# Splitting the experts' weights a whole 128x2048 unit at a time, with 8 KB places for the parts

## The chip, the cores and the metric

The kernel runs on one core of one Trainium2 chip. The metric is device time in microseconds (us) of one execution, and the median of the runs is compared. TensorE is called PE in the profile (PEld is its weight load), VectorE DVE, ScalarE ACT, GpSimd POOL; SP is the engine on whose queue the kernel issues its loads. The granted TensorE clock is 1.00 in nearly the whole profile; in the stretches of 5 us from 525 to 540 us, from the router into the experts, it is 0.65, 0.50 and 0.83.

## What is computed

Two layers of a decoder trunk for 256 tokens of width 1024, in float32. Layer 0 is a token mixer and a dense channel mixer; layer 1 is a token mixer and eight experts, of which each token takes two:

```python
def moe_swiglu(h, router_w, w_gate, w_up, w_down):
    t = h.reshape(B * S, D)
    logits = (t @ router_w).astype(jnp.float32)
    top_v, top_i = lax.top_k(logits, TOP_K)
    top_w = jax.nn.softmax(top_v, axis=-1)
    gates = jnp.sum(jax.nn.one_hot(top_i, N_EXPERTS) * top_w[..., None], axis=1)
    for e in range(N_EXPERTS):
        y = y + gates[:, e:e + 1] * swiglu(t, w_gate[e], w_up[e], w_down[e])
```

with `swiglu(h, g, u, d) = (silu(h @ g) * (h @ u)) @ d`, a width of 3584 inside, and a final RMSNorm. All weights are read once from HBM, 479 MB in all; the experts' are 336 loads of 1 MB.

## The kernel before, in words

**The products.** A float32 product is made of three products of float32r parts: with a weight w = hi + lo and an input x = hi + lo, PE does x_hi·w_hi, x_hi·w_lo and x_lo·w_hi. In the experts (`experts`, L854) the inputs are the stationary operand (128x128: `xe_hi`, `xe_lo` in `wide`, L990; `g_hi`, `g_lo` in `down`, L1028) and the weights are the moving one, 512 columns at a time. Each of the 8 experts is worked through in 7 chunks of 512 inner columns. A chunk is, in PE's order: the gate product (24 matmuls), with the turning of the chunk before put in after step k = 5 (`turn`, L1009: 4 transposes, then ACT's `g_hi` and DVE's `g_lo`); the up product (24); the down product of the chunk before (24). An expert's tokens are gathered ahead of it (`gather`, L968), its rows put back in small jobs (`finish`, L1046). The order within an engine is that of the code.

**The weights' way.** `Stream` (L81) brings them: `load` issues a load of one unit (128x2048 float32, 8 KB in each partition) when a load place is free; a unit holds two pieces of 1024 columns. `prep` has ACT copy a piece to its float32r part (L139: `w`, the hi); `rest` has DVE subtract it from the raw piece (L159: `lo`); when DVE has subtracted the last piece of a unit, the load place is free. A piece serves 6 matmuls. `get` hands out the next piece, and before that prepares ahead as far as places are free; `pump` prepares up to a number of pieces, with `lazy` their hi alone.

**The places.** Loads have 14 places of 8 KB in the experts: 8 of the pool `raws`, 3 of `raws2`, and the three tiles `q`, `k` and `v` of the pool `qkv`, which the mixer of layer 1 no longer needs (`ws.extend`, L788 and L791). Hi parts have 5 places of 4 KB: four of the pool `splits` and, since the mixer of layer 1, one of the pool `accs` (`ws.widen`, L1274); they are taken in turn, so that every fifth piece of the experts, beginning with the first, has its hi in `accs`. Lo parts have four of `splits`. The pools lie behind each other in memory in the order in which they are opened (L211 to L219, then L1278 on). In the built program the places of `splits` start 32 bytes past a multiple of 64, those of `accs` and the tiles `q`, `k` and `v` (all of the pools `accs` and `qkv`) at a multiple of 64. The stationary tiles of the experts (`xe_hi`, `xe_lo`, `g_hi`, `g_lo`) start 32 bytes past a multiple of 64, those of the dense mixer's down product and of the mixers (`dg_hi`, `dg_lo`, `onT_hi`, `onT_lo`) at a multiple of 64.

**The change over to the experts.** The mixer of layer 1 ends in `close` (L440), where `row_r` calls `ws.rest` (L460) just ahead of the second `diag`, which the transposes for the router wait for. In the router two pieces get their hi ahead (L929, L959); between them stands the branch of `overflow` (L1170), which all engines pass. `ws.rest(2)` (L962) stands in the middle of the eight subtractions of `xn[2]` (L964).

Of the kernel before, what the change touches and what calls it, by code (L numbers as in the profile page):

```python
# [44 lines left out]
# columns of the packed per-partition vectors, per layer  # L45
V_ADAB, V_ATTN, V_FFN, V_QN, V_KVN, V_OUT, V_FB = 0, 48, 56, 64, 66, 67, 75
V_LAYER = 76
# columns of the shape constants
# [6 lines left out]
# sections of the conditioning that are gates, the first section, and those whose sums wait for a time when  # L55
# the products' engine is free
# [6 lines left out]
# the channel blocks in the order in which they are modulated, those of a pair from different banks  # L63
NATURAL = ((0, 1), (2, 3), (4, 5), (6, 7))
PAIRS = ((0, 2), (1, 3), (4, 6), (5, 7))
# steps of the values' products that are followed by the first scores
# [13 lines left out]

class Stream:  # L81
    """Weights in the order of their use: loaded ahead, then split into two float32r parts.

    sources: of each unit, the address and the elements per partition. pieces: (unit, offset, what)
    in order, of SPLIT elements each; those with a `what` are folded into the conditioning instead."""

    def __init__(self, nc, sources, pieces, raw_pool, split_pool, fold):
        self.nc, self.sources, self.pieces = nc, sources, pieces
        self.raw_pool, self.split_pool, self.fold = raw_pool, split_pool, fold
        self.left = [0] * len(sources)  # L90
        for u, *_ in pieces:
            self.left[u] += 1
        self.raw, self.pool_of, self.bufs = {}, {}, RAW_BUFS
        self.loaded = self.oldest = self.next_prep = 0
        self.prepped = self.given = self.released = 0
        self.ready, self.late, self.late_by = [], [], 6
        self.turns, self.low_turns = ([(split_pool, tag, SPLIT_BUFS)] * SPLIT_BUFS for tag in ("whi", "wlo"))
        self.halves, self.held = [], {}

    def extend(self, raws):  # L100
        """Further places for loads, of pools and tags, which follow the others in turn."""
        for place in raws:
            self.pool_of[self.loaded] = place
            self.bufs += 1
            self.load()

    def widen(self, pool, tag):
        """A further place for a first part, which is the next in turn."""
        self.turns.insert(0, (pool, tag, 1))
# [14 lines left out]
    def prep(self, lazy=False):  # L124
        u, o, what = self.pieces[self.next_prep]
        self.load()
        raw = self.raw[u][:, o:o + SPLIT]
        i = self.next_prep
# [8 lines left out]
        else:  # L137
            hi = self.place(self.turns, f"w{i}")
# [4 lines left out]
            self.halves.append((u, raw, self.ready[-1]))  # L143
            self.prepped += 1

    def place(self, turns, name):
        turns.append(turns.pop(0))
        pool, tag, bufs = turns[-1]
        return pool.tile([P, SPLIT], F32R, tag=tag, name=name, bufs=bufs)

    def rest(self, n=None):
        """The second parts of the first n pieces that are ready: a step after the first parts, on
        another engine, which so need not wait for them."""
        n = len(self.ready) if n is None else n
        while (len(self.ready) - len(self.halves) < n and
               self.prepped - len(self.halves) < self.released + len(self.low_turns)):
            u, raw, parts = self.halves.pop(0)
            parts.append(self.place(self.low_turns, "lo"))
            self.nc.vector.tensor_sub(parts[1], raw, parts[0].bitcast(F32))  # L159
            self.used(u)  # L160
# [5 lines left out]
    def pump(self, most=None, need=0, lazy=False):  # L166
        """Prepare ahead: up to `most` pieces, as far as their places are free; lazy: only their first parts."""
        n = 0
        while self.next_prep < len(self.pieces) and (most is None or n < most):
            if self.pieces[self.next_prep][2] is None:  # L170
                ahead = len(self.turns) - (self.prepped >= self.given + need)
                if self.prepped >= self.released + ahead:
                    break
# [3 lines left out]
    def idle(self, most):  # L177
        """All uses of the pieces given have been issued; prepare some more."""
# [15 lines left out]
    def get(self, n=1):  # L194
        """The next pieces, once all uses of those given before have been issued."""
# [8 lines left out]


@with_exitstack
def trunk_kernel(ctx: ExitStack, tc: tile.TileContext, x, c, positions, w_early, w_moe, router_w,
# [5 lines left out]
    split_pool = ctx.enter_context(tc.tile_pool(name="splits", bufs=SPLIT_BUFS))  # L213
# [61 lines left out]
    def fold(w, l, section, k):  # L275
        """A part of a section of the conditioning: of the gates one row of eight, acc[p] += c[8 p + k] *
        w[8 p + k]; of the others a block of the channels, whose rows are the partitions. The blocks of
        the very first section are sums by the products' engine."""
        if (l, section) == FIRST:
            ps = bank("A", [P, P], "ps_fold")  # L280
            for i in range(KD):
                # a column and zeros: 128 columns cost less than one
# [9 lines left out]
        if k == 0:  # L292
            # the last may begin while the one before is held, after the last use of the conditioning's rows
# [9 lines left out]
        def done():  # L303
            """The sum over the partitions; what is returned puts it in its place."""
# [36 lines left out]
    for y in order:  # L341
        pieces.append((*place[y], y[1:] if y[0] == "ada" else None))
# [14 lines left out]
    def row_r(ss, n, name, between=None):  # L357
        """(sum of ss / n + eps) ** -0.5, of the rows' sums of squares; `between` goes where the
        vector engine waits for the last of them."""
# [17 lines left out]
    def turned(src, b, dg, ps, pairs=NATURAL):  # L377
        """The transpose of 128 rows times the diagonal, into PSUM [channel, 2, token] by pairs."""
# [24 lines left out]
    def modulated_T(l, at_g, sc, sh, ps, hi, lo):  # L403
        """The modulated rows, in two parts. Of each pair of blocks two engines make one each."""
# [15 lines left out]
    def first_modulated_T(ps, hi, lo, steps):  # L420
        """The very first of them, block after block as the conditioning comes in; steps: of how many
        blocks, and what brings theirs. The last parts of a step come after the folds of the next."""
# [17 lines left out]
    def close(l, section, acc, parts, n, table=None, spare=None, pairs=PAIRS, early=0):  # L440
        """x += gate row * acc, where parts(i, b, columns) are the last n steps of the sums acc[b];
        a quarter after the other, so that the next norm starts early. Its transpose and rstd. The sum
        of the held section `spare` goes where the products' engine waits for the last quarter."""
# [45 lines left out]
    def column_products(hT_hi, hT_lo, ps):  # L489
        """The next piece's products: [output channel, token]."""  # L490
# [4 lines left out]
    def first_products(hT_hi, hT_lo, pss, groups=PAIRS, late=False):  # L495
        """The next pieces' products, one for each of pss, as the blocks of the channels come in groups."""
# [18 lines left out]
    def mixer(l, pool, ps_x, loads=None, steps=None):  # L515
# [13 lines left out]
        def after():  # L529
            """Between the products: the next pieces' preparation, then a step of what goes on aside."""  # L530
# [7 lines left out]
        # of the query's two and of the keys' latent blocks  # L538
# [10 lines left out]
        def forget():  # L549
            """Cumulated logarithms of the forget gates, [head, token], as rows of the scores' factors;  # L550
            then the rotary part of the keys."""
# [66 lines left out]
        def score(g, h):  # L618
# [7 lines left out]
            for i, (c0, c1) in enumerate(((0, P), (P, 3 * P))):  # L626
                # -scale * (score + mask) and its least, -scale * the row's maximum
# [66 lines left out]
        # attention; the forgetting group first  # L694
# [12 lines left out]
        def weigh(g, h):  # L707
# [3 lines left out]
            # two heads wide, which costs no more; the next head puts its own over the second  # L711
# [21 lines left out]
        def group_T(g, between=None):  # L733
            """The group's rows turned; `between` goes after the first of its channel blocks."""
# [13 lines left out]
            # the two engines keep to different banks  # L748
# [24 lines left out]
        for i in range(len(AHEAD), n + 3):  # L773
# [8 lines left out]
            if i >= 3:  # L782
# [3 lines left out]
                if l and i == n + 2:  # L786
                    # of no further use here
                    ws.extend([(qkv_pool, "v")])  # L788
            if l and i == n - 1:
                ws.extend([(qkv_pool, "q"), (qkv_pool, "k")])  # L790
# [12 lines left out]
        ws.pump(2, need=2)  # L803
# [50 lines left out]
    def experts(l, outer, ps_x, rs):  # L854
        a = scale_of(l, V_FFN, 4, outer, "a_moe")
        # the normalised rows in three exact bfloat16 parts
# [15 lines left out]
        def pick(e):  # L872
            """Which token has which of the expert's slots, and the same turned."""
# [13 lines left out]
        with tc.tile_pool(name="route", bufs=1, reuse_waits="tile") as pool:  # L887
            # in places which take weights later
# [52 lines left out]
            # the slot of a token with its expert, or -1  # L941
# [5 lines left out]
            def gating():  # L947
                """The weights of the two experts of a token, [token, expert]."""
# [18 lines left out]
        with tc.tile_pool(name="moe", bufs=1, reuse_waits="tile") as pool:  # L967
            def gather(e, pk):  # L968
                """The expert's tokens, [channel, slot]; two channel blocks at a step."""
# [20 lines left out]
            def wide(e, ps):  # L990
                for k in range(KD):
                    xe_hi, xe_lo = xe[e][k]
                    c = halves[k % 2]
                    if k % 2 == 0:
                        hi, lo = ws.get()
# [7 lines left out]
            def step():  # L1003
                """The next of the small jobs that go on between the products."""
# [4 lines left out]
            def turn(pend):  # L1009
# [3 lines left out]
                if (e, ch) == (E - 1, CH - 1):  # L1013
                    # keeps clear of the parts in use
# [13 lines left out]
            def down(pend):  # L1028
# [3 lines left out]
                for f in range(NFC):  # L1032
                    hi, lo = ws.get()
# [12 lines left out]
            def finish(e):  # L1046
                """What is left of an expert, in small steps: its rows times the gate row, then onto their tokens."""
# [23 lines left out]
                # half by half: the second takes the places of the first's parts  # L1071
# [6 lines left out]
            def last_rows(e, fg):  # L1078
                """The last expert's rows onto their tokens, the final norm, and out."""
# [27 lines left out]
            for e in range(E):  # L1107
                for ch in range(CH):
# [22 lines left out]
                    parts = deque(slice(c, c + FC // 2) for c in (0, FC // 2))  # L1131
# [330 lines left out]
```

## Time and profile before

| | |
|---|---|
| median of 3 runs | 1531.49 us (1530.25 to 1533.41) |
| the profiled execution: span from first to last instruction | 1532.5 us |
| what lies around its span | not shown by itself; its span is 1.0 us above the median of the runs |
| PE / DVE / ACT busy in the span | 1501.3 us (98%) / 1304.3 us (85%) / 1072.6 us (70%) |
| the experts' products | from 533.5 us to 1521 us |
| DMA | 481.87 MB, mean 314 GB/s |

The profile is of one execution. A matmul's shown duration holds its way through the array, so that neighbouring ones overlap; what a matmul costs in a stream is the distance from its start to the start of the next.

### The profile page before, as it was taken

The numbers are of one execution on the slowest core, as the hardware profiler recorded it, in microseconds if no ns is written. First come the engines' busy times: TensorE is split into PE (matmuls) and PEld (weight loads), VectorE is DVE, ScalarE is ACT, GpSimd is POOL, SyncE is SP. The second block draws the span as 40 slices with busy tenths as digits, with TensorE's granted clock in tenths as the row PEclk, the third lists the DMA queues.
The fourth block names the chain that finished last, engine by engine and source line by source line (L and its number), as shares of the span: only waits on it lengthen the run. The fifth ranks groups of instructions, "written<-read, shape, count | busy, mean of one in ns | idle before, by whom it ended". The sixth has DMA issues, their size and how long they took to land.

```text
span 1532.5 us, 22473 instructions
## 1 busy us (share of the span) xinstructions
PE 1501.3 (98%) x8225; PEld 1271.6 (83%) x8225; DVE 1304.3 (85%) x1639; ACT 1072.6 (70%) x1468; POOL 12.6 (1%) x20
## 2 busy tenths in 40 slices
PE   7999999999999799999999999999999999999998
PEld 7988999999898678888888888888888888888886
DVE  5987877777876688899899889889989889988987
ACT  4575644444666578787787787787787778778775
POOL 1000000000000000000000000000000000000000
PEclk9999999999999899999999999999999999999999
DMA  9974778778573589999999999989989999999970
GB/s 367 401 278 165 290 281 310 293 279 316 192 252 112 192 302 358 359 364 360 371 339 359 377 340 361 367 336 358 382 333 370 362 357 353 355 381 336 358 285 28
DMA packets 68485, 481.87 MB, mean 314 GB/s; under 512 B 7953, under 2 KB 8593, under 8 KB 10770
## 3 DMA queue, kind: packets, MB, share of 16 engines
q1 hardware_dynamic: 68178, 480.33, 82.8%
q8 instruction: 66, 1.08, 0.3%
q14 instruction: 49, 0.40, 0.1%
q0 software_dynamic: 192, 0.05, 0.0%
HBM read 479.25 MB, written 1.05 MB: 313 GB/s over the span
## 4 chain that ended last, share of the span: by engine, by line
PE 64%; DVE 1%; issue 0%; ACT 0%; DVEq 0%
PE ps_up L997 20%; PE ps_gate L997 20%; PE ps_y L1040 20%; PE ps_gt L1023 2%; PE ps_g L978 1%; PE ps_sc L1066 0%; PE ps_sc L1067 0%; DVE xn L964 0%; DVE lo L159 0%; PE ps_sc L1090 0%; DVE fin L1098 0%; PE ps_b L881 0%; ACT junk L355 0%; ACT hf L984 0%; DVE x_sb L1092 0%
## 5 line engine op out<-in xcount | busy, mean ns | idle before, releaser
L159 DVE TENSOR_TENSOR lo<-raw,w 128x1024 fp32r<-128x1024 f32 x810 | 951.4, 1219 | 20.4 <-ACT w L139 16.6
L139 ACT ACTIVATE w<-raw 128x1024 fp32r<-128x1024 f32 x810 | 829.8, 1057 | 174.9 <-PE ps_gu L350 73.6
L997 PE MATMUL ps_gate<-w,xe_hi 128*128 128x512 f32 x448 | 181.7, 406 | 0.0
L997 PE MATMUL ps_up<-w,xe_hi 128*128 128x512 f32 x448 | 177.3, 396 | 0.0
L997 PE MATMUL ps_gate<-lo,xe_hi 128*128 128x512 f32 x448 | 175.9, 393 | 1.1 <-DVE lo L159 0.9
L997 PE MATMUL ps_gate<-w,xe_lo 128*128 128x512 f32 x448 | 175.9, 393 | 0.0
L997 PE MATMUL ps_up<-w,xe_lo 128*128 128x512 f32 x448 | 175.1, 391 | 0.0
L997 PE MATMUL ps_up<-lo,xe_hi 128*128 128x512 f32 x448 | 174.9, 390 | 0.0
L1040 PE MATMUL ps_y<-w,g_hi 128*128 128x512 f32 x440 | 138.2, 393 | 0.0
L1040 PE MATMUL ps_y<-lo,g_hi 128*128 128x512 f32 x440 | 137.4, 391 | 0.0
L1040 PE MATMUL ps_y<-w,g_lo 128*128 128x512 f32 x440 | 137.2, 391 | 0.0
L349 PE MATMUL ps_gu<-dT_hi,w 128*128 128x256 f32 x432 | 121.0, 280 | 0.0
L350 PE MATMUL ps_gu<-dT_lo,w 128*128 128x256 f32 x432 | 120.6, 279 | 0.0
L351 PE MATMUL ps_gu<-dT_hi,lo 128*128 128x256 f32 x432 | 120.5, 279 | 0.0
L400 ACT ACTIVATE g_hi<-ps_gt 128x512 fp32r<-128x512 f32 x55 | 33.0, 599 | 103.4 <-PE ps_gt L1023 103.4
L997 PEld LDWEIGHTS ps_gate<-lo,xe_hi 128*128 128x128 f32 x448 | 84.7, 189 | 19.1 <-DVE lo L159 3.1
L997 PEld LDWEIGHTS ps_gate<-w,xe_lo 128*128 128x128 f32 x448 | 84.4, 188 | 18.6
L997 PEld LDWEIGHTS ps_up<-lo,xe_hi 128*128 128x128 f32 x448 | 84.2, 188 | 18.6 <-DVE lo L159 0.6
L997 PEld LDWEIGHTS ps_up<-w,xe_lo 128*128 128x128 f32 x448 | 84.1, 188 | 18.5
L997 PEld LDWEIGHTS ps_up<-w,xe_hi 128*128 128x128 f32 x448 | 84.1, 188 | 17.3
L1040 PEld LDWEIGHTS ps_y<-lo,g_hi 128*128 128x128 f32 x440 | 82.5, 188 | 18.2 <-DVE lo L159 0.2
L997 PEld LDWEIGHTS ps_gate<-w,xe_hi 128*128 128x128 f32 x448 | 84.5, 189 | 15.7
(302 smaller groups left out, 2252.0 us busy)
## 6 DMA issues: line engine op xcount, KB each, us to landing
raw<-in_w_moe_dram SPq DMA_DIRECT2D x336, 1024.0 KB, 6.4
raw<-in_w_early_dram SPq DMA_DIRECT2D x114, 1024.0 KB, 7.0
raw<-in_w_early_dram SPq DMA_DIRECT2D x6, 512.0 KB, 7.8
gate<-in_ada_b_dram SPq DMA_DIRECT2D x4, 512.0 KB, 5.8
x_sb<-in_x_dram SPq DMA_DIRECT2D x1, 1024.0 KB, 7.7
out_dram<-fin SPq DMA_DIRECT2D x4, 256.0 KB, 2.1
fg<-in_final_g_dram SPq DMA_DIRECT2D x1, 512.0 KB, 3.8
cn<-in_consts_dram SPq DMA_DIRECT2D x1, 192.0 KB, 11.8
```

The source lines that it names most:

```text
L139: self.nc.scalar.activation(hi, raw, AF.Copy)
L159: self.nc.vector.tensor_sub(parts[1], raw, parts[0].bitcast(F32))
L349: nc.tensor.matmul(out_, lh, rh, start=start, stop=False)
L350: nc.tensor.matmul(out_, lh, rl, start=False, stop=False)
L351: nc.tensor.matmul(out_, ll, rh, start=False, stop=stop)
L400: nc.scalar.activation(hi, src, AF.Copy)
L978: nc.tensor.matmul(ps[:, j], part[:, b, (k0 + j) * P:(k0 + j + 1) * P], pk[:, b], start=(n == 0), stop=(n == 5))
L997: nc.tensor.matmul(ps, lh, w[:, c], start=(k == 0 and lh is xe_hi and w is hi), stop=(k == KD - 1 and lh is xe_lo))
L1023: nc.tensor.transpose(ps[:, i], act[:, (f0 + i) * P:(f0 + i + 1) * P], ident)
L1040: nc.tensor.matmul(y_ps[e][hf], lh, w[:, hf * 512:(hf + 1) * 512], start=(ch == 0 and f == 0 and lh is g_hi and w is hi), stop=(last and l ...
```

## The change

Units of the experts are split whole: one piece of the stream is a unit of 2048 columns, ACT and DVE each do one instruction for it, and `half` hands its two halves to the products. The tiles `q`, `k` and `v` no longer become load places: `q` and `k` become places for hi parts of 8 KB, `v` one for a lo part. The four 4 KB places of `whi` in `splits` are now one tile and count as two places of 8 KB after the mixer of layer 1, and likewise `wlo`. So the experts have 11 load places, 4 hi places (`q`, `k`, and two of `splits`) and 3 lo places (`v`, and two of `splits`), taken in turn from the first named; the place in `accs` is used no more after that mixer. In its last step one whole unit is prepared (`ws.pump(2 - l, need=2)`), where two pieces were. The product of silu and up is one instruction of 512 columns in place of two of 256.

```diff
+class Place:
+    def __init__(self, nc_tile, at=0):
+        self.tile, self.at, self.last = nc_tile, at, -1
...
-        self.turns, self.low_turns = ([(split_pool, tag, SPLIT_BUFS)] * SPLIT_BUFS for tag in ("whi", "wlo"))
+        self.split = [split_pool.tile([P, SPLIT_BUFS * SPLIT], F32R, name=name) for name in ("whi", "wlo")]
+        self.turns, self.low_turns = ([Place(t, i * SPLIT) for i in range(SPLIT_BUFS)] for t in self.split)
+        self.size, self.rest_of = SPLIT, []
...
+    def whole(self, high, low):
+        self.size = RAW
+        turns = []
+        for t, old, more in zip(self.split, (self.turns, self.low_turns), (high, low)):
+            new = [Place(x) for x in more]
+            for at in range(0, SPLIT_BUFS * SPLIT, RAW):
+                new.append(Place(t, at))
+                new[-1].last = max(x.last for x in old if x.tile is t and at <= x.at < at + RAW)
+            turns.append(new)
+        self.turns, self.low_turns = turns
...
+    def half(self):
+        if not self.rest_of:
+            hi, lo = self.get()
+            self.rest_of = [(hi[:, c:c + SPLIT], lo[:, c:c + SPLIT]) for c in range(0, hi.shape[-1], SPLIT)]
+        return self.rest_of.pop(0)
...
-        pieces.append((*place[y], y[1:] if y[0] == "ada" else None))
+        u, o = place[y]
+        if y[0] not in "gud":
+            pieces.append((u, o, SPLIT, y[1:] if y[0] == "ada" else None))
+        elif not o:
+            pieces.append((u, o, sources[u][1], None))
...
-                if l and i == n + 2:
-                    # of no further use here
-                    ws.extend([(qkv_pool, "v")])
-            if l and i == n - 1:
-                ws.extend([(qkv_pool, "q"), (qkv_pool, "k")])
...
-        ws.pump(2, need=2)
+        if l:
+            whi = [qkv_pool.tile([P, RAW], F32R, tag=tag, name="whi2") for tag in "qk"]
+            ws.whole(whi, [qkv_pool.tile([P, RAW], F32R, tag="v", name="wlo2")])
+        ws.pump(2 - l, need=2)
...
-                        hi, lo = ws.get()
+                        hi, lo = ws.half()
...
-                    parts = deque(slice(c, c + FC // 2) for c in (0, FC // 2))
+                    parts = deque([slice(0, FC)])
```

## Rows read from the trace of the kernel before

**Rows 1.** The page: its first line, and the chain that ended last by engine.

```profile
span 1532.5 us, 22473 instructions
...
PE 64%; DVE 1%; issue 0%; ACT 0%; DVEq 0%
```

**Rows 2.** Busy time by stretch: PE, PEld, DVE, ACT, POOL, clock, DMA share, GB/s.

```profile
900.00:1000.00 100.00, 100.00 (x451) 82.14 (x451) 93.16 (x99) 78.26 (x85) 0.00 (x0) 1.00 0.96 364
```

**Rows 3.** PE's waits from 556 to 1500 us: total us, times, longest.

```profile
PEld ps_gate L997 <- DVE lo L159: 0.6, 3, 0.2
PEld ps_y L1040 <- DVE lo L159: 0.2, 1, 0.2
PEld ps_up L997 <- DVE lo L159: 0.2, 1, 0.2
```

**Rows 4.** The waits of SP's DMA queue: total us, times, longest.

```profile
SPq L120 <- DVE lo L159: 893.5, 292, 19.1
```

**Rows 5.** Groups of instructions: count, busy us, mean ns of one, idle before.

```profile
L159 DVE TENSOR_TENSOR lo<-raw,w 128x1024 fp32r<-128x1024 f32 x810 | 951.4, 1219 | 20.4 <-ACT w L139 16.6 <-PE ps_w L350 2.6 <-issue 0.2
L139 ACT ACTIVATE w<-raw 128x1024 fp32r<-128x1024 f32 x810 | 829.8, 1057 | 174.9 <-PE ps_gu L350 73.6 <-PE ps_y L1040 43.2 <-PE ps_gate L997 13.7
...
L1061 DVE TENSOR_TENSOR y_lo<-yt,y_hi 128x512 fp32r<-128x512 f32 x14 | 9.6, 686 | 0.0
...
L1057 ACT ACTIVATE y_hi<-yt 128x512 fp32r<-128x512 f32 x14 | 8.8, 626 | 13.5 <-DVE yt L1053 13.5
```

**Rows 6.** Timeline from the mixer's end into the router: start, us, idle before.

```profile
504.71 1.22 DVE L159 TENSOR_TENSOR lo<-raw,w 128x1024 fp32r<-128x1024 f32 x1 [0.21 <-issue]
...
509.09 0.69 DVE L455 TENSOR_TENSOR gated<-ps_w,gate 128x512 f32<-128x512 f32 x1 [3.15 <-PE ps_w L351]
...
514.86 1.22 DVE L159 TENSOR_TENSOR lo<-raw,w 128x1024 fp32r<-128x1024 f32 x1
...
516.22 0.29 DVE L374 TENSOR_SCALAR diag<-cn,r_x 128x128 f32<-128x128 f32 x1
...
516.57 2.05 PE L381 MATMUL ps_nt<-diag,x_sb 128*128 128x128 f32 x16 [0.85 <-DVE diag L374]
...
525.04 2.23 ACT L139 ACTIVATE w<-raw 128x1024 fp32r<-128x1024 f32 x2
```

**Rows 7.** The branch at L1170 on PE's sequencer: ns, start.

```profile
L1170 PEldq COMPARE_BRANCH  x1: 3652/3652/3652, 525.1 to 525.1; - x1
```

**Rows 8.** Timeline of the experts' first two chunks, PE and DVE.

```profile
540.26 0.50 PE L997 MATMUL ps_gate<-lo,xe_hi 128*128 128x512 f32 x1 [0.53 <-DVE lo L159]
...
541.60 3.49 DVE L159 TENSOR_TENSOR lo<-raw,w 128x1024 fp32r<-128x1024 f32 x3
...
552.43 0.19 PEld L997 LDWEIGHTS ps_gate<-lo,xe_hi 128*128 128x128 f32 x1 [0.57 <-DVE lo L159]
```

**Rows 9.** Timeline of PE in the experts: the first matmul of five successive pieces.

```profile
994.81 0.39 PE L997 MATMUL ps_up<-w,xe_hi 128*128 128x512 f32 x1
...
996.17 0.39 PE L997 MATMUL ps_up<-w,xe_hi 128*128 128x512 f32 x1
...
997.56 0.40 PE L997 MATMUL ps_up<-w,xe_hi 128*128 128x512 f32 x1
...
998.97 0.61 PE L1040 MATMUL ps_y<-w,g_hi 128*128 128x512 f32 x2
...
1000.32 0.62 PE L1040 MATMUL ps_y<-w,g_hi 128*128 128x512 f32 x2
```

**Rows 10.** Timeline of PE, dense mixer: first of a piece's 12 matmuls, what follows.

```profile
176.91 0.39 PE L349 MATMUL ps_d<-w,dg_hi 128*128 128x512 f32 x1
...
179.71 0.28 PE L349 MATMUL ps_gu<-dT_hi,w 128*128 128x256 f32 x1
```

**Rows 11.** Timeline of PE, mixer of layer 1: piece with hi in `accs`, what follows.

```profile
496.76 0.39 PE L350 MATMUL ps_w<-lo,onT_hi 128*128 128x512 f32 x1
...
499.30 1.50 PE L381 MATMUL ps_nt<-diag,o_sb 128*128 128x128 f32 x12
```

More of the change, by code (lines that the diff above doesn't have):

```diff
@@ L88, in __init__ @@
         self.nc, self.sources, self.pieces = nc, sources, pieces
-        self.raw_pool, self.split_pool, self.fold = raw_pool, split_pool, fold
+        self.raw_pool, self.fold = raw_pool, fold
         self.left = [0] * len(sources)
@@ L105, in extend, with widen @@
             self.load()
-    def widen(self, pool, tag):
-        self.turns.insert(0, (pool, tag, 1))
+    def widen(self, tile_):
+        self.turns.insert(0, Place(tile_))
+    def whole(self, high, low):
[8 more added lines that the diff above has]
+        self.turns, self.low_turns = turns
     def load(self, most=None):
@@ L124, in prep @@
     def prep(self, lazy=False):
-        u, o, what = self.pieces[self.next_prep]
+        u, o, n, what = self.pieces[self.next_prep]
         self.load()
-        raw = self.raw[u][:, o:o + SPLIT]
-        i = self.next_prep
+        raw = self.raw[u][:, o:o + n]
         self.next_prep += 1
@@ L137, in prep @@
         else:
-            hi = self.place(self.turns, f"w{i}")
+            hi = self.place(self.turns, self.prepped, n)
             self.nc.scalar.activation(hi, raw, AF.Copy)
@@ L142, in prep, with place @@
             self.ready.append([hi])
-            self.halves.append((u, raw, self.ready[-1]))
+            self.halves.append((u, raw, self.prepped, self.ready[-1]))
             self.prepped += 1
[L146 to L149, printed above, removed]
+    def place(self, turns, i, n):
+        x = turns.pop(0)
+        turns.append(x)
+        assert x.last < self.released
+        x.last = i
+        return x.tile[:, x.at:x.at + n]
     def rest(self, n=None):
         n = len(self.ready) if n is None else n
[L155 to L158, printed above, removed]
+        while len(self.ready) - len(self.halves) < n and self.low_turns[0].last < self.released:
+            u, raw, i, parts = self.halves.pop(0)
+            parts.append(self.place(self.low_turns, i, raw.shape[-1]))
             self.nc.vector.tensor_sub(parts[1], raw, parts[0].bitcast(F32))
@@ L169, in pump @@
         while self.next_prep < len(self.pieces) and (most is None or n < most):
-            if self.pieces[self.next_prep][2] is None:
+            _, _, size, what = self.pieces[self.next_prep]
+            if what is None:
+                if size > self.size:
+                    break
                 ahead = len(self.turns) - (self.prepped >= self.given + need)
-                if self.prepped >= self.released + ahead:
+                if self.prepped >= self.released + ahead or self.turns[0].last >= self.released:
                     break
@@ L194, in get @@
     def get(self, n=1):
+        assert not self.rest_of
         self.settle()
@@ L212, in trunk_kernel @@
     raw_pool = ctx.enter_context(tc.tile_pool(name="raws", bufs=RAW_BUFS))
-    split_pool = ctx.enter_context(tc.tile_pool(name="splits", bufs=SPLIT_BUFS))
+    split_pool = ctx.enter_context(tc.tile_pool(name="splits", bufs=1))
     tiny = ctx.enter_context(tc.tile_pool(name="tiny", bufs=2))
@@ L1032, in down @@
                 for f in range(NFC):
-                    hi, lo = ws.get()
+                    hi, lo = ws.half()
                     g_hi, g_lo = g[f]
@@ L1272, in trunk_kernel @@
     gate_row(1, 5)
-    ws.widen(acc_pool, "acc")
+    ws.widen(acc_pool.tile([P, SPLIT], F32R, tag="acc", name="whi3"))
     with tc.tile_pool(name="mix1", bufs=1, reuse_waits="tile") as pool:
```

## The prediction, made before the changed kernel was run

> **What bounds the kernel now.** I read the page first. Its chain is PE for 64% of the span, more than any other engine [rows 1]; the reader is to see that DVE, which the change relieves, has 1% of it. Next the stretches: from 900 to 1000 us PE is busy all the time, DVE 93%, ACT 78%, and the DMA engines 96% [rows 2]. Three engines near their limit need the waits to tell which one sets the pace. PE's weight loads wait for DVE's `lo` only 1.0 us in all between 556 and 1500 us [rows 3], and SP's queue waits 893.5 us for `lo`, that is, for load places to come free [rows 4]. So DMA and DVE follow PE, and a faster DVE or ACT gains nothing in the experts. Only two things can move the time there: what a matmul costs in PE's stream, and the way into the stage.
>
> For the first I read PE's timeline, where the distances between starts are to be seen. A piece's six matmuls take 1.36 us from 994.81 (to 996.17) and 1.35 from 998.97 (to 1000.32), but 1.41 us (1.40 in most) from 997.56, and the piece ahead of that, from 996.17, 1.39 [rows 9]. The piece at 997.56 is number 315 of the experts, a multiple of five: its hi lies in `accs`, the others' in `splits`. No wait stands at these rows. So PE runs at two speeds, and a piece's place goes with them.
>
> **The change part by part.**
>
> *Splits.* 512 columns cost DVE 686 ns and 1024 cost 1219; ACT 626 and 1057 [rows 5]. Carried on by the same steps, 2048 columns are 1219 + 2 x 533 = 2285 ns on DVE, 1057 + 2 x 431 = 1919 ns on ACT (estimates). In a row three `lo` take 3.49 us [rows 8], 1.163 each, so a whole one costs about 2.23 against 2.33 for two. 336 times 0.10 is some 32 us off DVE, and 0: PE's matmuls hide it. If that cover were gone, the 1.0 us of waits [rows 3] could be gained.
>
> *One product of 512 columns.* One fixed cost less for DVE in each of 56 chunks, also under PE: 0. It begins at the time of the first half and is needed a whole chunk later, but for the last.
>
> *Three load places fewer.* The queue waits for places now [rows 4], so loads are early. A unit is two pieces of 1.36 to 1.41 us to PE [rows 9], some 2.75, so eleven places reach some 30 us ahead. 0. The cover is this reach; the DMA at 96% [rows 2] shows that it has little speed to catch up with, once late.
>
> *The lo at the mixer's end.* Now the first piece's `lo` runs at 504.71, ahead of an idle stretch of DVE of 3.15 us, and only the second's, at 514.86, stands before `diag` [rows 6]. A whole unit has its one `lo` at the second spot, where `row_r` calls `ws.rest`. It ends at 514.86 + 2.285 = 517.15 where `diag` began at 516.22, and PE waits for `diag` already 0.85 us [rows 6]. Everything up to the experts moves: +0.9 us. Bounds: 0, if the `lo` came earlier, and 1.1, the full extra length.
>
> *The lazy hi in the router.* ACT does two in 2.23 us [rows 6]; the first, whole, keeps ACT from the branch 0.86 us longer. PE's branch takes 3652 ns from 525.1 on [rows 7] and waits for no ACT: 0, at most 0.9. `ws.rest(2)` now has a `lo` to do (2.2 us) among the subtractions of `xn[2]`, behind the half that the first two gathers need: 0.
>
> *The first two chunks.* Here DVE is late, and PE waits for `lo` until 552.43 [rows 8]. From 541.60 to 552.4 (10.8 us) DVE did seven `lo` (7 x 1.163 = 8.1 us) and, the rest, 2.7 us of other work. Afterwards four whole ones lie ahead of the same matmul (8.9 us) with the same 2.7; they begin about 0.9 us earlier, since pieces 2 and 3 no longer have their `lo` at 539 us and one hi of 1.06 us no longer stands before the last `xe_hi` on ACT. 540.7 + 11.6 = 552.3: 0. Bounds: -2, if the waits all go, and +1.2, half a whole `lo`.
>
> *The places.* This is the largest term. In the dense mixer the four places of `splits` are slow as well: 12 matmuls in 179.71 - 176.91 = 2.80 us, 1.40 for six [rows 10]. So it isn't the pool alone. What fits all rows is the start within 64 bytes: fast where the weights and the stationary tile both begin 32 bytes past (experts with `splits`), slow where they differ (experts with `accs`; dense mixer with `splits`). `q`, `k` and `v` begin at a multiple of 64, like `accs`, their neighbour, while the experts' stationary tiles stay. I take them as slow. How it comes about no row shows.
>
> Before: 672 pieces, 134 slow by 0.04 us (5.4 us), and up to 0.03 more for the piece ahead of each (4.0). After: hi places go in fours, two slow, so 336 pieces x 0.04 = 13.4 us. Of the other 168 units one in three has its lo in `v`: 112 pieces at 0 to 0.04, so 0 to 4.5. In the mixer a piece whose hi alone agrees with the stationary tile takes (499.30 - 496.76) / 11 = 0.231 us a matmul [rows 11], between 0.227 and 0.233. Bounds: 13.4 - 9.4 = +4.0 and 17.9 - 5.4 = +12.5; I take the middle, +8.3.
>
> The Trainium skill, page "SBUF — State Buffer", section "SBUF: two separate sides", says that TensorE has ports of its own and never waits there for another engine; by that rule the place of a part costs nothing and this term is 0. The 1.40 against 1.36 us [rows 9] speaks against it, though the page doesn't speak of starts within 64 bytes.
>
> **The sum.** 0.9 + 0 + 8.3 = +9.2 us against the profiled execution: 1532.5 + 9.2 = 1541.7 us of span. The span is 1.0 above the median of the runs, so I add to the median: 1531.5 + 9.2 = 1540.7.
>
> **Rivals.** (1) *The new places are fast, and `accs` was slow for a reason of its own*, such as waits for another pool. For it: only one place of the experts was ever slow. Against it: the dense mixer's rows. Leaving `accs` gains 5.4 to 9.4 us against 0.9 lost: 1523 to 1527, say 1527.0. This is the other side; it decides once a piece with hi in `q` or `k` takes 1.36 us. (2) *Places cost what they cost before on average*, the speed being settled by what goes before on PE: only the router's 0.9 is left, 1532.4. The skill's rule named above would give the same. For it: the piece ahead of a slow one is slow too. (3) *Whole units come too late.* After a turn DVE stands behind `g_lo`, and the next `lo` is 1.1 us longer than a piece's. If PE waited 0.3 us in each of 56 chunks, +17, 1549; the full 1.1 each time would be +62. Against it: DVE has 0.1 us more room for each unit, 7% idle [rows 2], and the waits are 1.0 us in all [rows 3]. (4) *DMA can't keep up* with eleven places: a further form of being late, counted with (3).
>
> **Chances.** Likeliest case (slow `q`, `k`, `v`) 0.62, rival (1) 0.16, (2) 0.14, (3) and (4) 0.08. The likeliest alone runs from 0.9 - 2 + 4.0 to 1.1 + 1.2 + 12.5, 1534 to 1546 (without its extra 0.9 at the branch). The range for 8 in 10 takes in (2), the upper half of (1) and the edge of (3): 1526 to 1547. 0.2% is 3.1 us, about what a measurement of this kernel can tell from no change. Slower: the likeliest case less its lowest edge, and (3), 0.68. Same: (2) and that edge, 0.16. Faster: (1), 0.16.
>
> **What would show it.** In the profile after: PE's starts in pieces with hi in `q` and `k` 1.40 us apart for six, with hi and lo in `splits` 1.36; a stretch of 100 us holding some 1% fewer matmuls. `lo` 128x2048 near 2.29 us, hi near 1.92; a `lo` of that length just ahead of `diag`, and `diag` 0.9 us later. DVE's share in the experts down by 3 to 4 points with no gain in time. Waits of PE for `lo` after 556 us still near 1 us. Wrong if the pieces all take 1.36 us (then faster), or if PE's waits for `lo` in the experts exceed 5 us (then rival 3).

## The result, and the profile after

The changed kernel takes 1551.41 us (median of 4 runs, 1550.75 to 1551.72), the kernel before 1532.45 us beside it: a ratio of 1.0124 with a 95% interval of 1.0109 to 1.0138, 19.0 us slower. The prediction was 9.2 us slower, 1540.7 us, with 1547 as its upper end. The profiled execution has a span of 1549.3 us. It is 16.8 above that of before and not 19.0: its first `ps_v` product runs at 68.60 us, there at 70.60. That is scatter of the start and no effect of the change: over the 18 profiled executions of this document, of whatever kernel, this time lies between 68.33 and 70.69 us.

The page, its first line and the chain that ended last; then two lines of the groups of instructions by shape (count, busy us, mean ns of one, idle before):

```profile
span 1549.3 us, 21162 instructions
...
PE 62%; DVE 2%; ACT 1%; issue 0%; DMA 0%; DVEq 0%; ACTq 0%
```

```profile
L182 DVE TENSOR_TENSOR wlo<-raw,whi 128x2048 fp32r<-128x2048 f32 x336 | 756.6, 2286 | 22.2 <-ACT whi L161 22.2
...
L161 ACT ACTIVATE whi<-raw 128x2048 fp32r<-128x2048 f32 x336 | 625.9, 1912 | 50.6 <-PE ps_y L1077 49.9 <-PE ps_up L1034 0.6
```

The whole units cost what was worked out (2286 against 2285 ns, 1912 against 1919). The same stretch as in [rows 2], busy time by engine:

```profile
900.00:1000.00 100.00, 99.26 (x451) 80.48 (x449) 88.67 (x57) 72.22 (x52) 0.00 (x0) 1.00 0.94 356
```

DVE is down by 4.5 points, ACT by 6, and PE is no longer busy all the time. Where PE waits, from 556 to 1500 us (answers to [rows 3]):

```profile
PEld ps_y L1077 <- DVE wlo L182: 8.1, 7, 1.2
...
PE ps_y L1077 <- DVE wlo L182: 5.1, 7, 0.7
...
PEld ps_gate L1034 <- DVE wlo L182: 2.9, 7, 0.4
```

Each of these waits comes seven times, once for every expert but the first. The timeline of PE at the first of them, then that of DVE, then one line of ACT (start, us, idle before):

```profile
651.98 0.61 PE L1077 MATMUL ps_y<-whi,g_hi 128*128 128x512 f32 x2
653.33 0.73 PE L1077 MATMUL ps_y<-wlo,g_hi 128*128 128x512 f32 x2 [0.74 <-DVE wlo L182]
...
655.75 0.40 PE L1034 MATMUL ps_gate<-whi,xe_hi 128*128 128x512 f32 x1
656.13 0.50 PE L1034 MATMUL ps_gate<-wlo,xe_hi 128*128 128x512 f32 x1
```

```profile
640.74 2.28 DVE L182 TENSOR_TENSOR wlo<-raw,whi 128x2048 fp32r<-128x2048 f32 x1
644.47 0.42 DVE L439 TENSOR_TENSOR xe_lo<-hf,xe_hi 128x256 fp32r<-128x256 f32 x1 [1.45 <-ACT xe_hi L438]
646.39 0.43 DVE L439 TENSOR_TENSOR xe_lo<-hf,xe_hi 128x256 fp32r<-128x256 f32 x1 [1.50 <-ACT xe_hi L438]
646.74 2.29 DVE L182 TENSOR_TENSOR wlo<-raw,whi 128x2048 fp32r<-128x2048 f32 x1
649.34 0.43 DVE L439 TENSOR_TENSOR xe_lo<-hf,xe_hi 128x256 fp32r<-128x256 f32 x1 [0.32 <-ACT xe_hi L438]
650.65 0.42 DVE L439 TENSOR_TENSOR xe_lo<-hf,xe_hi 128x256 fp32r<-128x256 f32 x1 [0.88 <-ACT xe_hi L438]
650.99 2.28 DVE L182 TENSOR_TENSOR wlo<-raw,whi 128x2048 fp32r<-128x2048 f32 x1
```

```profile
646.27 1.90 ACT L161 ACTIVATE whi<-raw 128x2048 fp32r<-128x2048 f32 x1
```

These are the four steps of the next expert's gather. DVE stands idle 1.45 + 1.50 + 0.32 + 0.88 = 4.15 us for ACT's `xe_hi`, while the `lo` that begins only at 650.99 has had its hi since 646.27 + 1.90 = 648.17. PE wants it two matmuls after 651.98, at about 652.43, and gets it at 653.33; a second, smaller wait follows at 656.13. In the kernel before a `lo` of one piece stood between every two steps, and DVE was idle 1.13 + 0.55 + 0.55 + 0.56 = 2.79 us:

```profile
643.73 0.43 DVE L401 TENSOR_TENSOR xe_lo<-hf,xe_hi 128x256 fp32r<-128x256 f32 x1 [1.13 <-ACT xe_hi L400]
644.07 1.22 DVE L159 TENSOR_TENSOR lo<-raw,w 128x1024 fp32r<-128x1024 f32 x1
645.84 0.43 DVE L401 TENSOR_TENSOR xe_lo<-hf,xe_hi 128x256 fp32r<-128x256 f32 x1 [0.55 <-ACT xe_hi L400]
646.18 1.22 DVE L159 TENSOR_TENSOR lo<-raw,w 128x1024 fp32r<-128x1024 f32 x1
647.96 0.43 DVE L401 TENSOR_TENSOR xe_lo<-hf,xe_hi 128x256 fp32r<-128x256 f32 x1 [0.55 <-ACT xe_hi L400]
648.30 1.22 DVE L159 TENSOR_TENSOR lo<-raw,w 128x1024 fp32r<-128x1024 f32 x1
650.08 0.43 DVE L401 TENSOR_TENSOR xe_lo<-hf,xe_hi 128x256 fp32r<-128x256 f32 x1 [0.56 <-ACT xe_hi L400]
650.42 2.36 DVE L159 TENSOR_TENSOR lo<-raw,w 128x1024 fp32r<-128x1024 f32 x2
```

```profile
651.86 0.64 PE L1040 MATMUL ps_y<-lo,g_hi 128*128 128x512 f32 x2
```

There the first of the two at 650.42 was done only some 0.2 us before PE used it at 651.86: the margin at this spot was thin already.

PE's pace, for [rows 9]: the first matmuls of unit 84 (hi in `q`, lo in `v`), of 85, of 86 (both parts in `splits`), and of 87.

```profile
787.73 0.39 PE L1034 MATMUL ps_up<-whi,xe_hi 128*128 128x512 f32 x1
...
790.52 0.39 PE L1034 MATMUL ps_up<-whi,xe_hi 128*128 128x512 f32 x1
...
793.29 0.62 PE L1077 MATMUL ps_y<-whi,g_hi 128*128 128x512 f32 x2
...
796.02 0.62 PE L1077 MATMUL ps_y<-whi,g_hi 128*128 128x512 f32 x2
```

Twelve matmuls take 2.79 us in unit 84 and 2.73 in unit 86. Over all 4032 matmuls of the experts, leaving out distances above 262 ns (waits, turns), the mean distance from start to start is 228.79 ns before and 230.82 after.

**The account by trace.** From the experts' first matmul to their last: 987.45 us before, 1005.43 after, +18.0. Of it +8.2 is the pace (4032 x 2.03 ns); +9.2 is the stalls above (after 556 us, the distances longer than 326 ns between neighbouring matmuls exceed the pace by 0.3 us in all before, by 9.5 after); +0.4 is the first two chunks; the rest, 0.2, lies between the products. Ahead of the experts PE waits for the second `diag` 1.68 us, where it was 0.85 [rows 6]: +0.8. Together 18.8 of the 19.0 us.

```profile
512.99 2.28 DVE L182 TENSOR_TENSOR wlo<-raw,whi 128x2048 fp32r<-128x2048 f32 x1
515.19 0.28 DVE L412 TENSOR_SCALAR diag<-cn,r_x 128x128 f32<-128x128 f32 x1
515.52 2.05 PE L419 MATMUL ps_nt<-diag,x_sb 128*128 128x128 f32 x16 [1.68 <-DVE diag L412]
```

### The profile page after: what moved, and what is told of

Same layout as the page of the kernel before. It is cut to its first block, busy times and chain, and to the rows that moved or that the text cites. A ratio compares the mean times of both kernels' runs of the same rounds, so it can differ in the third digit from the quotient of the medians.

```text
span 1549.3 us, 21162 instructions
## 1 busy us (share of the span) xinstructions
PE 1512.2 (98%) x8225; PEld 1270.2 (82%) x8225; DVE 1280.9 (83%) x1247; ACT 1027.4 (66%) x1132; POOL 12.6 (1%) x20
## 4 chain that ended last, share of the span: by engine, by line
PE 62%; DVE 2%; ACT 1%; issue 0%; DMA 0%; DVEq 0%; ACTq 0%
PE ps_gate L1034 20%; PE ps_up L1034 19%; PE ps_y L1077 19%; PE ps_gt L1060 2%; DVE wlo L182 2%; PE ps_g L1015 2%; ACT hf L1021 0%; PE ps_sc L1103 0%; PE ps_sc L1104 0%; DMA raw<-in_w_moe_dram 0%; ACT xe_hi L438 0%; PE ps_sc L1127 0%; ACT whi L161 0%; DVE fin L1135 0%; ACT L1160 0%
## 5 line engine op out<-in xcount | busy, mean ns | idle before, releaser
L182 DVE TENSOR_TENSOR wlo<-raw,whi 128x2048 fp32r<-128x2048 f32 (+1 forms) x474 | 924.1, 1975 | 40.6 <-ACT whi L161 37.6
L161 ACT ACTIVATE whi<-raw 128x2048 fp32r<-128x2048 f32 (+1 forms) x474 | 770.3, 1663 | 153.1 <-PE ps_gu L388 73.8
L1034 PE MATMUL ps_gate<-whi,xe_hi 128*128 128x512 f32 x448 | 182.7, 408 | 0.0
L1034 PE MATMUL ps_up<-whi,xe_hi 128*128 128x512 f32 x448 | 178.0, 397 | 0.0
L1034 PE MATMUL ps_gate<-wlo,xe_hi 128*128 128x512 f32 x448 | 176.5, 394 | 0.7 <-DVE wlo L182 0.7
L1034 PE MATMUL ps_up<-wlo,xe_hi 128*128 128x512 f32 x448 | 176.3, 394 | 0.8 <-DVE wlo L182 0.8
L1034 PE MATMUL ps_gate<-whi,xe_lo 128*128 128x512 f32 x448 | 176.5, 394 | 0.0
L1034 PE MATMUL ps_up<-whi,xe_lo 128*128 128x512 f32 x448 | 175.8, 392 | 0.0
L1077 PE MATMUL ps_y<-wlo,g_hi 128*128 128x512 f32 x440 | 139.7, 396 | 5.4 <-DVE wlo L182 5.4
L1077 PE MATMUL ps_y<-whi,g_hi 128*128 128x512 f32 x440 | 139.1, 395 | 0.0
```

The lines of the kernel that those rows point to most:

```text
L161: self.nc.scalar.activation(hi, raw, AF.Copy)
L1034: nc.tensor.matmul(ps, lh, w[:, c], start=(k == 0 and lh is xe_hi and w is hi), stop=(k == KD - 1 and lh is xe_lo))
L1077: nc.tensor.matmul(y_ps[e][hf], lh, w[:, hf * 512:(hf + 1) * 512], start=(ch == 0 and f == 0 and lh is g_hi and w is hi), stop=(last and l ...
```

## The experiments

Ratios are those of a run to the kernel before, run beside it, with 95% intervals. The pace is the mean distance as above; the stage is from the start of the experts' first matmul to that of their last.

| run | us | ratio | pace, ns | stage, us |
|---|---|---|---|---|
| before | 1532.45 | | 228.79 | 987.45 |
| changed | 1551.41 | 1.0124 [1.0109, 1.0138] | 230.82 | 1005.43 |
| e1: changed, 32 bytes | 1558.51 | 1.0176 [1.0159, 1.0193] | 231.34 | 1006.86 |
| e2: changed, earlier lo | 1541.11 | 1.0065 [1.0048, 1.0082] | 230.84 | 995.67 |
| e3: both | 1549.95 | 1.0122 [1.0105, 1.0139] | 231.30 | 997.84 |
| e4: before, `accs` by 32 bytes | 1554.06 | 1.0145 [1.0128, 1.0161] | 232.49 | 1002.75 |
| f1: changed, 96 bytes | 1555.63 | 1.0148 [1.0131, 1.0165] | 231.17 | 1005.74 |
| f2: f1 with earlier lo | 1546.44 | 1.0093 [1.0076, 1.0110] | 231.15 | 996.82 |
| f3: before, `accs` by 96 | 1548.11 | 1.0105 [1.0088, 1.0122] | 232.23 | 1001.24 |
| f4: f2, mixers' tiles too | 1546.60 | 1.0098 [1.0082, 1.0115] | 231.13 | 996.48 |
| g1: changed, 224 bytes | 1537.84 | 1.0036 [1.0021, 1.0051] | 227.52 | 992.07 |
| g2: g1 with earlier lo | 1528.92 | 0.9979 [0.9969, 0.9988] | 227.53 | 983.92 |
| g3: before, `accs` by 224 | 1528.20 | 0.9973 [0.9963, 0.9983] | 227.43 | 982.58 |
| g4: g2, mixers' tiles too | 1531.94 | 0.9998 [0.9989, 1.0008] | 227.51 | 982.67 |
| h1: changed, product in halves | 1548.77 | 1.0102 [1.0086, 1.0117] | 230.84 | 1002.86 |
| h2: before, eleven load places | 1532.57 | 0.9999 [0.9990, 1.0009] | 228.80 | 987.60 |
| h3: g2 with two more edits | 1527.24 | 0.9961 [0.9947, 0.9975] | 227.48 | 983.63 |
| h4: g3 with one more edit | 1526.51 | 0.9962 [0.9949, 0.9976] | 227.41 | 981.78 |

**The places, first try (e1, e4) and the stall (e2, e3).** Small unused tiles shift what lies behind them:

```diff
+    qkv_pool.tile([P, 8], F32, name="pad_q")
+    mixer_pool.tile([P, 8], F32, name="pad_m")
     rope_t = mixer_pool.tile([P, S], F32, name="rope_t")
...
+        outer.tile([P, 8], F32, name="pad_o")
         a = scale_of(l, V_FFN, 4, outer, "a_moe")
```

> The changed kernel with 32 bytes put ahead of q, k and v (and as many again ahead of two later pools, so that the experts' stationary tiles keep their starts): all places of hi and lo parts in the experts now begin 32 bytes past a multiple of 64, as the stationary tiles do. Theory (a piece is slow where its start and that of the stationary tile differ within 64 bytes): the mean distance of PE's starts falls from 230.9 to about 227.3 ns, 4032 x 3.6 ns = 14.5 us less, so about 1537 us; the stalls of 1.3 us once in an expert stay. Rival (the pace does not depend on starts, but on what goes before, or q, k and v are slow as memory of another pool): 1551 us as before the edit, and the mean stays at 230.9 ns.

The earlier lo:

```diff
                     for k in wide(e, pu):
+                        if k == 5 and ch == CH - 1:
+                            ws.rest(2)
                         if k % 2:
                             next(ahead, None)
```

> The changed kernel with the lo of the unit after next issued ahead of the third step of each gather (one call of rest) and not behind the fourth. Theory (seven times, DVE stands behind the gather's xe_lo while the lo that PE needs next could have run): the waits of 1.13 + 0.33 and 0.39 + 0.34 us go, seven times about 1.3 us, 9 us less: about 1542 us. Rival (DVE has not the speed at that place, since a whole lo takes 2.29 us): the wait only moves to the xe_lo of the next expert or to the next unit, and the time stays within 2 us of 1551. Rival (eleven load places are too few): the same, 1551, since DMA is not touched.

> Both edits, the 32 bytes and the earlier lo. Theory: the two add up, 14.5 + 9 us less than 1551, about 1528 us, some 4 us below the kernel before. If a faster PE finds DVE late, up to 5 us of it are lost: 1533. By the rivals of both: 1551.

In e4 the tile of 32 bytes stands first in `accs`, and a second first in `qkv`, so that `q`, `k`, `v` and all behind them move by 64.

> The kernel before, with only its place in accs moved by 32 bytes (q, k and v, load places here, and all stationary tiles keep their starts within 64 bytes). Theory: every piece of the experts is now fast, the mean distance falls from 228.9 to about 227.3 ns, 4032 x 1.6 = 6.4 us less: about 1525.5 us. Rival (accs is slow for its pool, not for its start): 1531.5, every fifth piece still 1.40 us.

e2 came out as the theory had it: 10.3 us less. DVE's timeline there, at the same gather:

```profile
642.83 0.42 DVE L439 TENSOR_TENSOR xe_lo<-hf,xe_hi 128x256 fp32r<-128x256 f32 x1 [1.45 <-ACT xe_hi L438]
644.76 0.42 DVE L439 TENSOR_TENSOR xe_lo<-hf,xe_hi 128x256 fp32r<-128x256 f32 x1 [1.50 <-ACT xe_hi L438]
645.10 4.49 DVE L182 TENSOR_TENSOR wlo<-raw,whi 128x2048 fp32r<-128x2048 f32 x2
649.50 0.75 DVE L439 TENSOR_TENSOR xe_lo<-hf,xe_hi 128x256 fp32r<-128x256 f32 x2
```

The second `lo` now fills what was idle, nothing else comes late for it, and no wait of PE for `wlo` is left between 556 and 1500 us. DVE had the speed; its order was the cause.

e1 and e4 went the wrong way, by 7.1 and some 22 us. Some 5 us of each lie ahead of the experts, where the mixers' tiles had moved by 64 bytes too; most of it is the dense mixer's 1344 products of 256 columns, whose mean distance rose from 116.8 ns to 120.0 in e1 and 119.9 in e4. In the experts e1 is 1.4 us longer than the changed kernel and e4 15.3 longer than the kernel before. A shift that made all starts agree within 64 bytes slowed PE: the starts matter, but not by that rule. e3 shows the same on top of e2: 8.8 us above it. In e4 the pieces of `splits`, whose own starts had not moved, had become slow, as the distances over six matmuls show, each from the fourth matmul of a piece to that of the next (1.40 us):

```profile
1006.02 0.39 PE L999 MATMUL ps_up<-w,xe_hi 128*128 128x512 f32 x1
...
1007.42 0.39 PE L999 MATMUL ps_up<-w,xe_hi 128*128 128x512 f32 x1
...
1008.82 0.39 PE L999 MATMUL ps_up<-w,xe_hi 128*128 128x512 f32 x1
```

What had moved, by 64 bytes, was the stationary tile. So the remainder that counts is not that of 64.

**Second try, 128 bytes (f1 to f4).** The same edits with 24 floats in place of 8 in `qkv` (f1, f2) or `accs` (f3), the others staying at 8; f4 without the tile in the mixer's pool.

> The changed kernel with 96 bytes put ahead of q, k and v, and 32 ahead of two later pools, so that q, k, v, splits and the experts' stationary tiles all start 96 bytes past a multiple of 128. Theory, mended after the first four runs (moving part and stationary tile must start at the same place within 128 bytes, not 64; the 32-byte edit made q, k and v agree but moved the stationary tiles away from splits): the mean distance of PE's starts falls from 230.9 to about 227.4 ns, 14 us less, about 1537 us; the stalls of 1.3 us in an expert stay. Rival (starts within 128 bytes are as little the cause as those within 64; any shift disturbs the pace): not below 1549.

> The same with the earlier lo at the gathers, which took 10.3 us off by itself. Theory: 14 + 10.3 us less than 1551.4, about 1527 us, below the kernel before. If a faster PE finds DVE late, up to 1532. Rival: 1541 as with the earlier lo alone.

> The kernel before with its place in accs alone moved to 96 bytes past a multiple of 128, like splits and the stationary tiles, which stay. Theory: the slow fifth of the pieces goes, mean distance 228.9 to about 227.3 ns, 6 us less: about 1525.5 us. Rival (accs slow for its pool): 1531.6.

> The second of these with the stationary and moving tiles of both mixers and the dense mixer also at 96 bytes past a multiple of 128 (no 32 bytes ahead of the mixer's pool). Theory: the down product of the dense mixer, some 336 matmuls, and the mixers' products of 512 columns lose 6 ns each, about 3 us; its 1344 matmuls of 256 columns are unknown, 0 to 6 ns each, up to 8 us. About 1522 us, between 1516 and 1525. Rival: as the second.

All four missed: f1 is 4.2 us slower than the changed kernel, though its stage is only 0.3 us longer; the rest lies ahead of the experts. With ten traces at hand, each matmul's distance could be sorted by what the built kernels say of the starts of its moving part and its stationary tile, modulo 256. Here are the experts' matmuls that have the same difference as their seven neighbours in the stream:

```
difference of starts, modulo 256    matmuls    mean distance, ns
  0                                   4157       227.3
 32                                    560       233.3
128                                   3338       232.8
192                                   2775       233.4
```

Which neighbours are counted moves these means by up to 0.7 ns; the gap of over 4 ns stays. Modulo 512, the group 0 splits into 0 and 256, which differ by 1 ns at most. The dense mixer's down product, also of 512 columns, adds differences that no expert matmul had: 233.1 ns at 224 (kernel before), 233.6 at 160 (e1), 233.2 at 96 (f1). A difference of 64 occurs at 512 columns in no run. Among the starts of the two kernels compared in the prediction only the differences 0 and 32 occur in the experts, and these look the same modulo 64, 128 and 256.

**Third try, 256 bytes (g1 to g4).** 56 floats (224 bytes) in `qkv` (g1, g2, g4) or `accs` (g3). g4 lacks the tile in the mixer's pool, so that the tiles of the mixers and of the dense mixer move to 224 as well.

> The changed kernel with 224 bytes ahead of q, k and v and 32 ahead of two later pools: q, k, v, splits and the experts' stationary tiles all start 224 bytes past a multiple of 256. Theory, mended again from the ten traces: sorted by whether moving part and stationary tile start at the same place within 256 bytes, matmuls amid neighbours that all agree stand 227.3 ns apart, amid neighbours that all differ 233.1 (the earlier edits of 32 and 96 bytes made some places agree and others differ). The mean distance falls from 230.9 to about 227.4 ns: 14 us less, about 1537 us; the stalls of 1.3 us in an expert stay. Rival (any shift of the tiles disturbs the pace, and the sorting only mirrors it): 1549 us or more, as with 32 and with 96 bytes.

> The same with the earlier lo at the gathers. Theory: 14 + 10.3 us less than 1551.4, about 1527 us; up to 1532 if a faster PE finds DVE late. Rival: 1544 or more, as with 96 bytes and the earlier lo.

> The kernel before with its place in accs at 224 bytes past a multiple of 256, like splits and the experts' stationary tiles, which keep their starts within 256. Theory: all pieces of the experts agree, mean distance 228.9 to about 227.3 ns, 6 us less: about 1525.5 us. Rival: 1548 or more, as with 96 bytes.

> The second of these with the tiles of both mixers and of the dense mixer also at 224 past a multiple of 256 (the same place as splits, where their weights lie). Theory: the dense mixer's 336 matmuls of 512 columns and the mixers' some 190 lose 6 ns each, 3 us, and the products of 256 columns 0 to 6 ns each, 0 to 15 us for some 2500: between 1509 and 1524 us. Rival (the rule holds only for the experts): 1527.

g1 fell to 1537.84 us, 13.6 less than the changed kernel where 14 were expected; g2 and g3 are below the kernel before (g3's 3.9 us at a stage 4.9 shorter, where 6 were expected). The units 84 to 86 and the start of 87 in g1:

```profile
785.05 0.39 PE L1037 MATMUL ps_up<-whi,xe_hi 128*128 128x512 f32 x1
...
787.77 0.39 PE L1037 MATMUL ps_up<-whi,xe_hi 128*128 128x512 f32 x1
...
790.49 0.62 PE L1080 MATMUL ps_y<-whi,g_hi 128*128 128x512 f32 x2
...
793.21 0.62 PE L1080 MATMUL ps_y<-whi,g_hi 128*128 128x512 f32 x2
```

2.72 us each, in whatever place. g4 missed: 3.0 us slower than g2. The dense mixer's products of 512 columns gained (mean distance 233.1 to 229.1 ns), but its 1344 of 256 columns, whose moving part is `dT`, lost (116.7 to 119.8 ns, 4.2 us in all). Two groups of g4, then of g2 (count, busy, mean ns):

```profile
L389 PEld LDWEIGHTS ps_gu<-dT_lo,whi 128*128 128x128 f32 x432 | 82.9, 192 | 1.2 <-issue 0.2
...
L389 PE MATMUL ps_d<-wlo,dg_hi 128*128 128x512 f32 x112 | 43.9, 392 | 0.0
```

```profile
L390 PEld LDWEIGHTS ps_gu<-dT_lo,whi 128*128 128x128 f32 x432 | 81.2, 188 | 1.4 <-issue 0.2
...
L390 PE MATMUL ps_d<-wlo,dg_hi 128*128 128x512 f32 x112 | 44.3, 396 | 0.0
```

So the rule holds for 512 moving columns, and not for 256. There the difference alone doesn't sort the speeds at all: 116.8 ns at 32 and 119.8 at 0, but also 120.0 at 96 (e1), and at 160 once 118.6 (f1) and once 117.4 (f3). What does stays open.

**Which part made the order late, and what is left (h1 to h4).** h1 restores `parts = deque(slice(c, c + FC // 2) for c in (0, FC // 2))`; h2 takes both calls of `ws.extend` with `q`, `k` and `v` out of the kernel before. h3 and h4 get 224 bytes ahead of the dense mixer's `dg`, and h3 an early `lo`:

```diff
+            if not j:
+                pool.tile([P, 56], F32, name="pad_d")
             g_hi = pool.tile([P, S], F32R, name="dg_hi", bufs=LAST + 1)
...
         ws.pump(2 - l, need=2)
+        if l:
+            ws.rest()
```

> The changed kernel with the product of silu and up in two instructions of 256 columns again. Theory (the once-in-an-expert stall comes from the order of lo and the gather's xe_lo, and the product has no part in it): the same stalls, 1551 us within 1. Rival (the one instruction of 512 comes later than the first of two and pushes the lo behind it): the stall shrinks and the time falls by up to 9 us.

> The kernel before with q, k and v no longer load places: eleven in place of fourteen, all else as it was. Prediction and theory: 0, 1532 us within 1, PE's waits for lo in the experts as before, about 1 us. Rival (eleven places don't reach far enough, and a load late by some us stops ACT and DVE): 1535 or more, with waits for DMA.

> The changed kernel with 224 bytes and the earlier lo at the gathers (1528.9 us), and two more edits: the dense mixer's stationary dg at 224 past a multiple of 256, like its weights (its moving dT stays at 0), and the first whole lo issued right behind its hi, ahead of DVE's idle stretch of 4.58 us, and not ahead of diag. Theory: 336 matmuls times 4 to 6 ns are 1.3 to 2 us; the wait of PE for the second diag falls from 1.68 to 0.85 us: together 2 to 3 us less, about 1526.5. Rival (other work moves into the gap): 1529.

> The kernel before with accs at 224 past a multiple of 256 (1528.2 us) and the dense mixer's dg there too. Theory: 1.3 to 2 us less, about 1526.5, the same as the changed kernel with all four edits: in the experts, where PE sets the pace, whole units gain nothing. Rival (whole units gain some us once all places agree, since DVE has more room): this one is slower than that by over 2 us.

h1 is 2.6 us below the changed kernel, where the theory had no change; its rival had up to 9 and came true in part. Its stall has lost the second part. PE's waits there:

```profile
PEld ps_y L1077 <- DVE wlo L182: 8.1, 7, 1.2
...
PE ps_y L1077 <- DVE wlo L182: 5.1, 7, 0.7
...
PEld ps_gate L1034 <- DVE wlo L182: 0.3, 2, 0.2
```

The long distances exceed the pace by 7.6 us in place of 9.5. After the late `lo` the changed kernel's DVE takes the whole product ahead of the next `lo`, which PE then meets at `ps_gate`; with two halves that one is in time. So the one product has 1.9 of the 9.2 us, and what is left, 7.3, goes with the whole units. h2 shows the load places at no cost, as predicted; nor does any wait of PE, DVE or ACT that the view shows in the changed kernel's experts, from 533 to 1525 us, end with a load. In h3 DVE's `lo` ahead of `diag` is gone:

```profile
513.69 0.15 DVE L404 SCALAR_TENSOR_TENSOR rs_m<-ss,eps 128x1 f32<-128x1 f32 x1
515.13 0.29 DVE L414 TENSOR_SCALAR diag<-cn,r_x 128x128 f32<-128x128 f32 x1 [1.28 <-ACT r_x L409]
```

and PE's wait for this `diag` is back at 0.85 us, where g2 still has 1.68. The dense mixer's down product, whose stationary tiles now start where its weights do, runs at 229.1 ns (h3) and 228.9 (h4) in place of 233.1, which is 1.3 us. In all h3 is 1.7 us below g2, where 2 to 3 were expected. h3 and h4 are 0.4% below the kernel before, and not to be told from each other (1526.36 to 1529.63 us against 1525.94 to 1528.50): with agreeing places whole units show no gain and no loss, and DVE's relief buys nothing where PE sets the end.

## Why the prediction was wrong

- **What bounds the kernel** was right: by the page DVE's busy time fell from 1304.3 to 1280.9 us and ACT's from 1072.6 to 1027.4, and no time came back for it (h3 against h4).
- **The places** came out in size, +8.2 where +8.3 was predicted, but by a rule that was wrong as it stood, and so close by luck: +8.3 was the middle of a range from 4.0 to 12.5. Starts within 64 bytes fitted every row of before, since no row could tell 64 from 256; e1, e4 and f1 to f4 refuted it, g1 and g3 bore out 256. "It begins at a multiple of 64" gave the right verdict on `q`, `k` and `v` only because they also differ from the stationary tiles by 32 modulo 256. The Trainium skill, page "SBUF — State Buffer", section "A bandwidth-pool intuition that's wrong (but worth ruling out)", gives PE a second, independent read port for weight loads. By that alone one would look for no cost in the relation of the two starts, though the page doesn't speak of starts. The measurement decides: 227.3 against 233 ns. How the cost comes about stays open.
- **The router's `lo`** was right: PE's wait for `diag` grew by 0.83 us, 0.9 predicted. The branch cost nothing, as predicted.
- **The first two chunks**, put at 0, cost 0.4 us.
- **Load places** at 0: right (h2).
- **The step that failed** is "*Splits* ... and 0: PE's matmuls hide it", with "*One product* ... also under PE: 0". The cover was taken from DVE's mean busy share and from waits summed over the stage. It was thin at the seven gathers (0.2 us at the one shown), where DVE's order ties `lo` to ACT's `xe_hi`, and halving the number of `lo` there took away two of four places where work stood in the gaps. That cost 9.2 us, of which the product has 1.9. The prediction's own sign of this, waits for `lo` over 5 us, came true: 8.1 + 2.9 us at PE's weight loads. Rival (3), "whole units come too late", named the mechanism, but behind the turn of each of 56 chunks; it was behind the gathers, 7 times 1.3 us. The timelines of DVE and PE at one gather of the kernel before would have shown it.

## What to carry to other kernels

A queue's mean reserve says little about an instruction order: before merging small instructions of an off-path engine into large ones, look in the timeline at the places where that engine also waits for others, and count what used to stand in those gaps. Once work is merged, put the call that issues it ahead of the wait, and the loss is gone (e2). And where matmuls stream without waits at two speeds, sort them by the starts of both operands in memory before blaming a pool, and try the remainder at more than one power of two; a few unused bytes took 13.6 us off here (g1), and the merging itself took nothing off (h3 against h4).

## What was not expected of the hardware

- The distance of 512-column matmuls, each with a weight load of its own, was 227.3 ns where moving part and stationary tile start at the same place modulo 256 bytes, and 232.8 to 233.4 ns at differences of 32, 128 and 192. Slow matmuls also slow their neighbours: where both kinds are mixed, matmuls whose own starts agree stood 228.9 (kernel before) to 231.6 ns (f3) apart.
- With 256 moving columns equal starts were not the fast ones: 116.8 ns at a difference of 32, and 119.8 ns where the starts agree (g4), with weight loads of 192 in place of 188 ns. A difference of 96 was as slow, 120.0 ns (e1).
